# One core, a two-layer trunk in split float32: padded arrays, common splits, one turned K tile, and low parts that lag

## The chip, the cores and the metric

The kernel runs on one core of a Trainium2 chip. The metric is the device time of one execution in microseconds, and the runs shown are 2053.0, 2053.09 and 2053.85 us, a median of 2053.09 us. The profile is of one further execution.

## The reference, cut to what matters

256 tokens of width 2048 go through two layers. Layer 0 mixes with a short gated convolution, layer 1 with latent attention; each is followed by an MLP of width 8192, and each of the four sub-layers ends in a layer norm.

```python
def short_conv_mixer(x, w_in, conv_w, w_out):
    gate_b, gate_c, u = jnp.split(x @ w_in, 3, axis=-1)
    y = conv(gate_c * u, conv_w)                # depthwise, width 3, causal
    return (gate_b * y) @ w_out
def sq_relu_mlp(x, w1, w2):
    return jnp.square(jax.nn.relu(x @ w1)) @ w2
# per layer: h = LN(ALPHA*h + mix(h)); h = LN(ALPHA*h + sq_relu_mlp(h))
# layer 1's mix: multi-head latent attention, 16 heads, output projection w_o (2048 x 2048)
```

All inputs and the output are float32.

## The kernel before, in words

**Split products.** TensorE's one-pass float32 format drops bits, so each operand is split into a high part, which that format holds exactly, and a low part, the rest (`split`, L109 to L112: a cast on ScalarE, a subtraction on VectorE). A product needs high x high, high x low and low x high. Activations lie in SBUF as [128, 512] tiles per K tile: 256 columns of high parts, then 256 of low parts.

**Unit.** In `w_in`, `w_out`, `w_o` and `W1` a unit is one 128-wide block of output features over all 16 K tiles. Per K tile it issues two matmuls: `high` (L190) holds the weights' high part and streams 512 columns, `low` (L194) holds the weights' low part and streams 256. `mm_run` (L196) issues them in turn, h0 l0 h1 l1 and so on to h15 l15. One unit needs two stream halves of 512 KB. `products` (L230) yields the units; the convolution has 48, of which the first three run as a group that starts while data arrive, `w_out` has 16, `w_o` 16 (three in a group `first_o`, between the heads of attention), and each of W1's eight quarters q (`mlp`, L523) has 8 units. Quarter 0 uses another form (`mm_wide`, three 258-column matmuls per K tile, which fold in the layer norm).

**Down projection.** W2 is computed per quarter with the hidden activations as weights of TensorE and the rows of W2 as the 512-column moving operand. `down` (L259) does three matmuls per K tile, token half and column block (`dot`, L245 to L249). In the quarters of `FAST` (1 to 6 in layer 0, 1 to 7 in layer 1) half of the columns use a form with 7 instead of 8 block products (`down_fast`, L287), which needs sums of hidden blocks, `forms` (L566 to L574), and sums of weight blocks (`prepare`, L150 to L165).

**Order.** Weights are loaded by SyncE's queue (L132), split, and used; `take` (L171) runs `LOOK` = 5 halves ahead, with 5 raw buffers and 8 buffers each for high and low halves. A scheduler behind the tile framework fixes the order on each engine, and semaphores do the rest. PSUM has 8 banks.

**Where the arrays lie.** SBUF tiles follow each other in the order in which their pools were filled, rounded up to 32 bytes. Worked out from the sizes per partition: 16384 bytes of DMA scratch and 128 of constants, then `vec` 736, `cos_t` and `sin_t` 1024 each, `mask_t` 1536, `id_t` and `ones` 512 each, `col` 16 (32), `xres` 16384, and then the arrays a1 (16512), a2 (16512), b (33024) and c (16384), and behind them the raw, high and low buffers of 4096 each. So by 512 bytes a1 starts at remainder 384, a2 at 0, b at 128, c and all weight buffers at 384, and the small array `t4` of the fast form at 256. The convolution's input is in a1 and a2, its result z, W1's input and attention's output oT are in b, the hidden activations in c, the forms in a2.

**The hidden activations.** Per unit `hidden` (L558) evacuates PSUM, applies relu and square, and splits the 256 columns into `h` at once (`put_split`, L306). After each odd unit four subtractions and additions make the forms of the pair, which are split in turn (512 columns).

**The end.** In the last quarter of layer 1, `to_out` (L866) loads the norm's gain and bias, broadcast to all partitions, in four transfers of 512 KB (`gbt`, L869, GpSimd's queue). The array takes the place of W1's input, so they wait for the last W1 unit.

Of the kernel before, what the change touches and what calls it, by code (L numbers as in the profile page):

```python
# [15 lines left out]
P = 128  # L16
# [24 lines left out]

C_G, C_B, C_CW, C_QG, C_KG, C_END = 0, 64, 128, 176, 180, 184
# [3 lines left out]
def trunk(ctx: ExitStack, tc: tile.TileContext, xT, vecs, w_in, w_out, w_kv, w_q, w_uk, w_uv,  # L46
# [10 lines left out]


# [137 lines left out]
    def mm_run(wps, x, k0, k1, nk, tiles_first=False):  # L196
# [33 lines left out]
    def products(n, x, group=0, cuts=()):  # L230
# [20 lines left out]
    def held(x, t):  # L251

        return [x[:, o + t * P:o + (t + 1) * P] for o in (0, T)]
# [33 lines left out]
    def down_fast(x, forms):  # L287
# [3 lines left out]
        for j in range(n):  # L291
            b, = take(1)
            a = {"11": held(x[2 * j], 0), "12": held(x[2 * j + 1], 0), "22": held(x[2 * j + 1], 1)}
            for i in range(4):
                a[f"S{i + 1}"] = [forms[:, j, o, i * P:(i + 1) * P] for o in range(2)]
# [16 lines left out]
    vec = const.tile([P, C_END], F32, name="vec")  # L312
# [5 lines left out]
    col = const.tile([P, 4], F32, name="col")  # L318
# [28 lines left out]
    class Norm:  # L347
# [35 lines left out]
        def widen(self, *tags):  # L383
# [4 lines left out]
            for i, tag in enumerate(tags):  # L388
                x = act.tile([P, n, 2 * W], F32R, tag=tag, name=f"xd{self.idx}_{i}")
# [85 lines left out]
    xhl = [t[:, k, :] for t in [act.tile([P, NC // 2, 2 * T], F32R, tag=a, name=f"xhl0_{a}") for a in ("a1", "a2")]  # L475
           for k in range(NC // 2)]

    first = act.tile([P, 2 * GROUP, 1024], F32, tag="b", name="first")
# [14 lines left out]
    zt = act.tile([P, NC, 2 * T], F32R, tag="b", name="z")  # L493
    z = [zt[:, k, :] for k in range(NC)]
    cbuf = act.tile([P, 2, 5, T + 2], F32, tag="c", name="cbuf")
# [27 lines left out]
    def mlp(idx, ln, begin, blocks, fast):  # L523
# [3 lines left out]
        xt = act.tile([P, NC, 2 * T], F32R, tag="b", name=f"xhl{idx}")  # L527
# [20 lines left out]
        for q in range(NQ):  # L548
            ht = act.tile([P, QC, 2 * T], F32R, tag="c", name=f"h{idx}_{q}")
            h = [ht[:, k, :] for k in range(QC)]  # L550
            forms = None
            if q in FAST[idx // 2]:
                forms = act.tile([P, QC // 2, 2, 4 * P], F32R, tag="a2", name=f"forms{idx}_{q}")
            if q == NQ - 1:
                begin(block)
            pair = []

            def hidden(m, ps, evac, *func):  # L558
                f = tmp.tile([P, T], F32, tag="fh", name="fh", bufs=3)
# [4 lines left out]
                put_split(h[m], f)  # L564
                pair.append(f)
                if forms is not None and m % 2:  # L566
                    (a11, a21), (a12, a22) = ((v[:, :P], v[:, P:]) for v in pair[-2:])
# [417 lines left out]
```

## Time and profile before

| What | Value |
|---|---|
| Median of the runs | 2053.09 us |
| Profiled execution: span | 2049.4 us |
| Around the span, median less span | 3.7 us |
| TensorE busy | 2030.6 us (99%), 11208 matmul records |
| VectorE busy | 1662.8 us (81%) |
| ScalarE busy | 1194.1 us (58%) |
| DMA | 385.32 MB, 188 GB/s over the span |
| Granted TensorE clock, mean | 0.997 |

The matmul records overlap: a 512-column matmul has a record of some 390 ns but the next one starts some 230 ns later. So the busy share of TensorE says nothing about its pace; that is read from the starts of successive matmuls, either in the timeline or as the first and last start of the matmuls of one line in a stage, divided by the number of steps between them.

### The profile page before, as it was taken

Reading aid. Unit: us, or ns where it says so; the run is one execution under the profiler, and the core shown is the slowest. Engines: PE = TensorE matmul, PEld = TensorE weight load, DVE = VectorE, ACT = ScalarE, POOL = GpSimd, SP = SyncE. Lnnn points to the kernel's source line nnn. Section 1 sums busy time; section 2 is a strip of 40 time slices with the busy share of each in tenths; the row PEclk is TensorE's granted clock in tenths of the full one; section 3 lists DMA queues with packets and bytes.
Section 4 is the critical chain, followed back from the end, with each engine's and each line's share of the span. In section 5 each row is a group of like instructions: output and inputs, shape, how many; then the busy total and the mean of one; then the engine's idle time right before and its main releaser. Section 6 shows DMA issues by size and latency. Waiting matters only on the chain.

```text
span 2049.4 us, 30194 instructions
## 1 busy us (share of the span) xinstructions
PE 2030.6 (99%) x11208; PEld 1760.4 (86%) x11208; DVE 1662.8 (81%) x2602; ACT 1194.1 (58%) x1860; POOL 4.5 (0%) x25
## 2 busy tenths in 40 slices
PE   9999999999999999999999999999999999999997
PEld 8888888988888888888889998898888888888885
DVE  7667677678898988989788878776879888898988
ACT  6444445676566565655656665566656656566562
POOL 0000000000000000000000000000000000000000
PEclk9999999999999999999999999999999999999998
DMA  8666666564746557465755544656475664756653
GB/s 308 202 188 187 186 185 194 159 211 136 249 142 223 193 167 250 143 226 173 234 169 164 166 124 142 197 174 196 138 236 161 196 218 156 243 153 217 212 165 137
DMA packets 108003, 385.32 MB, mean 188 GB/s; under 512 B 11984, under 2 KB 13392, under 8 KB 107856
## 3 DMA queue, kind: packets, MB, share of 16 engines
q1 hardware_dynamic: 107136, 381.04, 58.7%
q0 software_dynamic: 576, 2.10, 0.3%
q8 instruction: 88, 1.44, 0.3%
q14 instruction: 59, 0.48, 0.1%
q10 hardware_dynamic: 144, 0.26, 0.0%
HBM read 381.25 MB, written 2.10 MB: 187 GB/s over the span
## 4 chain that ended last, share of the span: by engine, by line
PE 97%; DVE 1%; DMA 1%; issue 0%; ACT 0%; SPq 0%; DVEq 0%
PE ps_u L190 34%; PE ps_u L194 17%; PE ps_d L248 7%; PE ps_d L247 7%; PE ps_d L249 7%; PE ps_f L249 4%; PE ps_f L248 4%; PE ps_f L247 4%; PE ps_w L224 1%; PE ps_w L222 1%; PE ps_w L223 1%; PE ps_g L222 1%; PE ps_g L224 1%; PE ps_g L223 1%; PE ps_wo L190 1%; PE S L788 1%
## 5 line engine op out<-in xcount | busy, mean ns | idle before, releaser
L112 DVE TENSOR_TENSOR lo<-raw,hi 128x1024 fp32r<-128x1024 f32 x712 | 861.7, 1221 | 299.0 <-ACT hi L111 294.3
L111 ACT CAST hi<-raw 128x1024 fp32r<-128x1024 f32 x712 | 742.2, 1049 | 526.6 <-PE ps_u L190 289.5
L190 PE MATMUL ps_u<-xhl,hi 128*128 128x512 f32 x1792 | 632.2, 398 | 0.0
L194 PE MATMUL ps_u<-xhl,lo 128*128 128x256 f32 x1792 | 503.0, 281 | 0.0
L190 PEld LDWEIGHTS ps_u<-xhl,hi 128*128 128x128 f32 x1792 | 336.5, 188 | 82.3
L194 PEld LDWEIGHTS ps_u<-xhl,lo 128*128 128x128 f32 x1792 | 338.5, 189 | 0.5
L190 PE MATMUL ps_u<-xhl_a,hi 128*128 128x512 f32 x720 | 253.4, 396 | 0.0
L248 PE MATMUL ps_d<-lo,h 128*128 128x512 f32 x608 | 236.9, 390 | 0.0
L249 PE MATMUL ps_d<-hi,h 128*128 128x512 f32 x608 | 236.8, 390 | 0.0
L247 PE MATMUL ps_d<-hi,h 128*128 128x512 f32 x608 | 236.6, 389 | 0.0
L194 PE MATMUL ps_u<-xhl_a,lo 128*128 128x256 f32 x720 | 202.9, 282 | 0.0
L190 PEld LDWEIGHTS ps_u<-xhl_a,hi 128*128 128x128 f32 x720 | 135.2, 188 | 31.9
L194 PEld LDWEIGHTS ps_u<-xhl_a,lo 128*128 128x128 f32 x720 | 135.8, 189 | 0.0
L248 PEld LDWEIGHTS ps_d<-lo,h 128*128 128x128 f32 x608 | 114.1, 188 | 24.2 <-DVE lo L112 0.4
L247 PEld LDWEIGHTS ps_d<-hi,h 128*128 128x128 f32 x608 | 114.2, 188 | 24.0
L249 PEld LDWEIGHTS ps_d<-hi,h 128*128 128x128 f32 x608 | 114.1, 188 | 23.9
L111 ACT CAST hi_t<-raw_t 128x1024 fp32r<-128x1024 f32 x52 | 54.8, 1054 | 77.8 <-PE ps_u L190 41.8
L190 PE MATMUL ps_u<-z,hi 128*128 128x512 f32 x256 | 89.0, 392 | 0.0
L562 ACT ACTIVATE fh<-fh 128x256 f32<-128x256 f32 x112 | 46.4, 414 | 72.0 <-DVE fh L304 72.0
L222 PE MATMUL ps_w<-xd,hi 128*128 128x258 f32 x256 | 72.5, 284 | 0.0
L224 PE MATMUL ps_w<-xd,hi 128*128 128x258 f32 x256 | 72.5, 285 | 0.0
L223 PE MATMUL ps_w<-xd,lo 128*128 128x258 f32 x256 | 72.3, 282 | 0.0
(235 smaller groups left out, 3254.8 us busy)
## 6 DMA issues: line engine op xcount, KB each, us to landing
raw<-in_w_dram SPq DMA_DIRECT2D x408, 512.0 KB, 4.4
raw<-in_w2f_dram SPq DMA_DIRECT2D x104, 512.0 KB, 3.6
raw<-in_w_in_dram SPq DMA_DIRECT2D x90, 512.0 KB, 4.2
raw<-in_w_out_dram SPq DMA_DIRECT2D x32, 512.0 KB, 3.6
raw<-in_w_o_dram SPq DMA_DIRECT2D x32, 512.0 KB, 3.9
raw<-in_w_kv_dram SPq DMA_DIRECT2D x10, 512.0 KB, 4.3
raw<-in_w_q_dram SPq DMA_DIRECT2D x8, 512.0 KB, 4.5
raw<-in_w_uk_dram SPq DMA_DIRECT2D x8, 512.0 KB, 4.4
```

The lines of the kernel that those rows point to most:

```text
L111: nc.scalar.copy(hi, src)
L112: nc.vector.tensor_tensor(lo, src, hi.bitcast(F32), ALU.subtract)
L190: nc.tensor.matmul(ps, w[blk // 8][0][:, blk % 8, :], x, start=first, stop=False)
L194: nc.tensor.matmul(ps[:, :T], w[blk // 8][1][:, blk % 8, :], x[:, :T], start=False, stop=last)
L222: nc.tensor.matmul(ps[:, :W], hi, x[k][:, :W], start=k == 0, stop=False)
L223: nc.tensor.matmul(ps[:, :W], lo, x[k][:, :W], start=False, stop=False)
L224: nc.tensor.matmul(ps[:, :W], hi, x[k][:, W:], start=False, stop=k == NC - 1)
L247: nc.tensor.matmul(ps, x[0], w[0], start=first, stop=False)
L248: nc.tensor.matmul(ps, x[0], w[1], start=False, stop=False)
L249: nc.tensor.matmul(ps, x[1], w[0], start=False, stop=last)
L562: nc.scalar.activation(f, f, AF.Relu)
L788: nc.tensor.matmul(S[:, at:at + n], qp[:, tok], kp[:, :n], start=False, stop=True)
```

## The change

- `array` gives a1, a2, b and c rounded-up sizes (16896, 16896, 33280, 16384 bytes), `vec` and `col` are padded to 1024 and 512 bytes, `stats` to 320, and the DMA scratch shrinks from 16384 to 2048 bytes. By the same sum a1, a2, b, c, the weight and raw buffers, `t4` and the pair buffer `sf` all start at remainder 128 by 512 bytes.
- In the quarters 1 to 7 the relu and square of two units go into one pair buffer `sf` of 1024 columns, the four sums stand behind them there, and one split makes all 8 blocks (4 in layer 0's last quarter): high parts in c, low parts in a2. Nothing is split before the odd unit of a pair.
- In the first unit of each of these quarters the low matmul of K tile 2 stands before the high one: h0 l0 h1 l1 l2 h2 h3 l3.
- In the ungrouped units of the convolution, of `w_out` and of `w_o`, `mm_lag` issues h0 to h7, then h8 l0 h9 l1 to h15 l7, then l8 to l15.
- The four `gbt` transfers go to SyncE's queue.

```diff
+COL = 128
+LAG = 8
+    ROOM = {"a1": 16896, "a2": 16896, "b": 33280, "c": 16384}
+    def array(tag, dtype, name, *dims):
+        n = int(np.prod(dims))
+        t = act.tile([P, ROOM[tag] // 4], dtype, tag=tag, name=name)[:, :n]
...
         for k, (w, ps) in order:
+            if k == turn:
+                low(ps, w, k, x[k], False)
+                high(ps, w, k, x[k], False)
+                continue
             high(ps, w, k, x[k], k == 0)
             low(ps, w, k, x[k], k == nk - 1)
+    def mm_lag(ps, w, x):
+        for k in range(NC + LAG):
+            if k < NC:
+                high(ps, w, k, x[k], k == 0)
+            if k >= LAG:
+                low(ps, w, k - LAG, x[k - LAG], k == NC + LAG - 1)
...
-            mm_run([(w, ps)], x, 0, NC, NC)
+            if lag:
+                mm_lag(ps, w, x)
+            else:
+                mm_run([(w, ps)], x, 0, NC, NC, turn=turn if i == 0 else None)
...
+            forms = [array(a, F32R, f"h{idx}_{q}_{a}", QC // 2, 8 * P) for a in ("c", "a2")] if q else None
...
+                    if m % 2 == 0:
+                        state["pair"] = fast.tile([P, 8 * P], F32, tag="sf", name="sf")
+                    f = state["pair"][:, m % 2 * T:(m % 2 + 1) * T]
...
-                put_split(h[m], f)
...
+                    split(hi[:, :cols], lo[:, :cols], src[:, :cols])
...
-                for m, ps in enumerate(products(QC, xhl)):
+                for m, ps in enumerate(products(QC, xhl, turn=2, lag=False)):
...
-            nc.gpsimd.dma_start(gbt[:, n, :], gb[n].partition_broadcast(P))
+            nc.sync.dma_start(gbt[:, n, :], gb[n].partition_broadcast(P))
...
-    nc = _bacc.Bacc("TRN2", target_bir_lowering=False, num_devices=1)
+    nc = _bacc.Bacc("TRN2", target_bir_lowering=False, num_devices=1, dynamic_dma_scratch_size=2048)
```

More of the change, by code (lines that the diff above doesn't have):

```diff
@@ L294, in down_fast @@
             for i in range(4):
-                a[f"S{i + 1}"] = [forms[:, j, o, i * P:(i + 1) * P] for o in range(2)]
+                a[f"S{i + 1}"] = [v[:, j, (4 + i) * P:(5 + i) * P] for v in forms]
             for p, l, r in FACTORS:
@@ L523, in mlp @@
     def mlp(idx, ln, begin, blocks, fast):
-        xt = act.tile([P, NC, 2 * T], F32R, tag="b", name=f"xhl{idx}")
+        xt = array("b", F32R, f"xhl{idx}", NC, 2 * T)
         xhl = [xt[:, k, :] for k in range(NC)]
```

72 lines of the change are left out of this document (39 added, 33 removed).

## The prediction

> **What bounds the kernel now.** I read the page first: shares, chain, groups. In the chain's line the shares are of the span.
>
> ```profile
> span 2049.4 us, 30194 instructions
> PE 2030.6 (99%) x11208; PEld 1760.4 (86%) x11208; DVE 1662.8 (81%) x2602; ACT 1194.1 (58%) x1860; POOL 4.5 (0%) x25
> ...
> PE 97%; DVE 1%; DMA 1%; issue 0%; ACT 0%; SPq 0%; DVEq 0%
> ```
>
> TensorE is 97% of the chain, so hardly anything is to be had from waits, and time can only come from the pace at which matmuls follow each other. I therefore read the timeline of PE in two stages that do the same work: units of W1 in a middle quarter and in the last quarter of layer 0.
>
> ```profile
> 474.22 0.40 PE L190 MATMUL ps_u<-xhl,hi 128*128 128x512 f32 x1
> 474.46 0.28 PE L194 MATMUL ps_u<-xhl,lo 128*128 128x256 f32 x1
> 474.58 0.40 PE L190 MATMUL ps_u<-xhl,hi 128*128 128x512 f32 x1
> ...
> 475.28 0.40 PE L190 MATMUL ps_u<-xhl,hi 128*128 128x512 f32 x1
> ```
> ```profile
> 990.00 0.39 PE L190 MATMUL ps_u<-xhl,hi 128*128 128x512 f32 x1
> 990.23 0.28 PE L194 MATMUL ps_u<-xhl,lo 128*128 128x256 f32 x1
> 990.35 0.39 PE L190 MATMUL ps_u<-xhl,hi 128*128 128x512 f32 x1
> 990.58 0.28 PE L194 MATMUL ps_u<-xhl,lo 128*128 128x256 f32 x1
> 990.69 0.39 PE L190 MATMUL ps_u<-xhl,hi 128*128 128x512 f32 x1
> ```
>
> ```profile
> 458.70:503.90 45.20, 45.20 (x258) 39.18 (x256) 35.10 (x55) 28.67 (x50) 0.00 (x0) 1.00 0.44 138
> 978.00:1022.60 44.60, 44.60 (x259) 39.32 (x258) 32.16 (x49) 27.48 (x46) 0.00 (x0) 1.00 0.69 225
> ```
>
> The first column of the timeline is the start; the last three of the two stretches are granted clock, DMA share and GB/s. In the first stage three K tiles take 475.28 - 474.22 = 1.06 us, 353 ns each; in the second two take 0.69 us, 345 to 347 ns each. Same lines, arrays and shapes, clock at 1.00 in both: there are two **gaits**, a slow and a fast one. The rows of whole stages (count, then first and last start of L190) tell which stage has which: W1's second quarter in layer 0, its seventh and its last in layer 1, a stretch of the convolution, the most of `w_out`, and `w_o`.
>
> ```profile
> L190 PE MATMUL ps_u<-xhl,hi x128: 389/398/403, 458.7 to 503.5; 128*128 128x512 f32 x128
> L190 PE MATMUL ps_u<-xhl,hi x128: 389/398/403, 1856.1 to 1901.0; 128*128 128x512 f32 x128
> L190 PE MATMUL ps_u<-xhl,hi x128: 391/391/476, 1946.0 to 1990.2; 128*128 128x512 f32 x128
> L190 PE MATMUL ps_u<-xhl_a,hi x257: 387/396/403, 63.8 to 153.9; 128*128 128x512 f32 x129
> L190 PE MATMUL ps_u<-z,hi x209: 391/391/391, 295.0 to 367.1; 128*128 128x512 f32 x105
> L190 PE MATMUL ps_u<-oT,hi x208: 392/394/395, 1260.4 to 1332.2; 128*128 128x512 f32 x104
> ```
>
> Per K tile: 44.8/127 = 352.8 and 44.9/127 = 353.5 ns (I take 353.1); 44.2/127 = 348.0 with a disturbed first one in it; 90.1/256 = 352.0; 72.1/208 = **346.6**; 71.8/207 = 346.9. The six middle quarters of each layer come straight from 512-column matmuls of the down projection and keep the slow gait through all 128 K tiles. The two last quarters come from other matmuls (a mean, L365; transposes, L863) and keep the fast one. So the gait depends on how a stage is entered, and it lasts.
>
> Three more rows give the pace of one kind alone: 512 columns in the down projection (every third matmul is L248), 512 columns in the fast form (first matmuls of its four K pairs, 21 apart), and 256 columns (every third is L208).
>
> ```profile
> L248 PE MATMUL ps_d<-lo,h x64: 387/389/389, 415.4 to 458.2; 128*128 128x512 f32 x64
> L247 PE MATMUL ps_f<-t,h x4: 392/392/393, 503.9 to 518.5; 128*128 128x512 f32 x4
> L208 PE MATMUL ps_k<-lat,lo x16: 280/283/285, 1124.5 to 1129.9; 128*128 128x256 f32 x16
> ```
>
> 42.8/189 = **226.5** ns, 14.6/63 = **231.7** ns, 5.4/45 = **120** ns. And 226.5 + 120 = 346.5: the fast gait is the sum of the two kinds alone. I take that as the floor; no row is below it. The down projection has both operands at remainder 384 by 512 bytes; the fast form mixes weights of TensorE at 384 and 0 with moving operands at 384 and 256, and is 5.2 ns slower per matmul.
>
> **The change part by part.**
>
> *Turned K tile.* In 12 quarters the swap breaks the alternation after two K tiles. Price: none in instructions; both ends are zero (the gait is not left) and (353.1 - 346.6) x 126 x 12 = 9.8 us gained. Of the entries of other kinds that I see, W1's last quarters, `w_out` and `w_o` ended in the fast gait, the convolution in a slow one. I take the gain, **-9.5 us** with the first tiles left slow.
>
> *Padding.* With everything at remainder 128, the fast form should run as the down projection does, whose operands also agree. 84 matmuls x 5.2 ns x 12 blocks = 5.2 us; a few matmuls at each entry stay slow, **-5.0 us**. Both operands at 128 is in no row. But z and W1's input lie at 128 against weights at 384 and reach the floor, the down projection has 384 against 384 and is on it too, so I expect 128 and 384 to be alike. Bounds: 0, and -5.5.
>
> *Lag.* Eight h, then eight pairs, then eight l. At the floor it is the same sum as before, 8 x 226.5 + 8 x 346.6 + 8 x 120. The eight pairs are entered from 512-column matmuls, as W1's slow quarters are, so I price them slow: 8 x 6.5 = 52 ns, less some 7 because the first pair after such an entry is short, 45 ns a unit. The convolution now loses (352.0 - 346.6) x 16 = 86 ns in each of 45 units: gain 45 x 41 = 1.9 us. `w_out` and `w_o` lose nothing now: 29 x 45 = 1.3 us more. Net **-0.6 us**; bounds: all fast, -3.9; all 74 units as slow as W1, 74 x 104 ns - 3.9 = +3.8. The high matmul of the last K tile also comes 1.0 us earlier in the unit (8 x 226.5 + 7 x 346.6 = 4.2 us after its start, not 15 x 0.35), and `w_out`'s first unit needs z[15] there:
>
> ```profile
> 281.34 1.05 ACT L111 CAST hi<-raw 128x1024 fp32r<-128x1024 f32 x1 [1.40 <-PE ps_u L190]
> ...
> 283.57 0.42 DVE L309 TENSOR_TENSOR z<-cbuf,z 128x256 fp32r<-128x256 f32 x1
> ```
>
> The split that ends z stands behind a weight cast that waits for a high buffer and behind that weight's subtraction. With high parts first that buffer comes free about 0.9 us earlier, and in the new order on VectorE the z row stands ahead of that subtraction (1.2 us). So z[15] comes 1 to 2 us earlier too, and I take 0; without this cover it costs 1.0 us, once. Low buffers come free up to 1.8 us later; with 8 of them, four units' worth, nobody waits.
>
> *Common splits.* Per pair of hidden units ScalarE and VectorE each do one 1024-column split in place of three, and TensorE waits on none of it: the last pair is needed 63 matmuls, 14.3 us, after the last unit. In layer 0's last quarter it is needed 36 matmuls, 8.2 us, after it, and is ready now about 5.7 us after it:
>
> ```profile
> L309 DVE TENSOR_TENSOR h<-fh,h x2: 418/418/418, 1022.3 to 1027.9; 128x256 fp32r<-128x256 f32 x2
> ```
>
> The pair's split adds some 0.5 us: 2 us of cover, price **0**. The single pair buffer is rewritten behind the subtraction that reads it, on the same engine.
>
> *The gain and bias on another queue.* This is the one real stall. Rows: the chain of waits (load, start and length), the page (median of such loads), the timeline of VectorE, PE, GpSimd and SyncE, two stretches, then the block's own rows.
>
> ```profile
> 1993.17 8.60 DMA raw<-in_w2f_dram
> ```
> ```profile
> raw<-in_w2f_dram SPq DMA_DIRECT2D x104, 512.0 KB, 3.6
> ```
> ```profile
> 2001.80 1.23 DVE L154 TENSOR_TENSOR raw_t<-raw,raw 128x1024 f32<-128x1024 f32 x1 [3.39 <-DMA raw<-in_w2f_dram]
> 2002.94 0.28 DVE L573 TENSOR_TENSOR sf<-fh,sf 128x128 f32<-128x128 f32 x1
> ...
> 2005.61 0.68 DVE L112 TENSOR_TENSOR forms<-sf,forms 128x512 fp32r<-128x512 f32 x1
> ...
> 2006.15 0.50 PE L247 MATMUL ps_f<-t,h 128*128 128x512 f32 x1 [0.78 <-ACT t L111]
> 2008.08 0.55 PE L248 MATMUL ps_f<-t,h 128*128 128x512 f32 x1 [1.44 <-DVE t L112]
> ...
> 1990.99 2.23 POOL L869 DMA_DIRECT2D gbt<-in_gb_dram  x4 [1038.46 <-PE ps_u L194]
> 1988.47 5.03 SPq L132 DMA_DIRECT2D raw<-in_w2f_dram  x2
> ...
> 1993.00:2002.00 9.00, 9.00 (x41) 7.22 (x40) 5.07 (x10) 3.55 (x6) 0.21 (x1) 1.00 0.99 366
> 2008.00:2011.60 3.60, 3.52 (x9) 2.80 (x10) 3.41 (x4) 1.04 (x1) 0.00 (x0) 0.55 0.81 277
> ...
> L247 PE MATMUL ps_f<-t,h x4: 393/395/497, 1990.5 to 2006.1; 128*128 128x512 f32 x4
> ...
> L247 PE MATMUL ps_d<-hi,h x1: 389/389/389, 2014.4 to 2014.4; 128*128 128x512 f32 x1
> ```
>
> The last weight load of the fast form takes 8.6 us instead of 3.6, because the four transfers share the DMA engines with it (366 GB/s, share 0.99). TensorE waits for what is made of it, and then runs at half clock. The block lasts from 1990.5 to 2014.4, 23.9 us, where the same block takes 14.6/63 x 84 = 19.5: 4.4 us lost. After the change the four stand ahead of that load on SyncE. They wait for the same last unit (1991.0), and at 0.33 us each (the load's issue, 1993.17 to 1993.50) are out by 1992.3, before the load itself may start, so this wait delays nobody. 2.10 + 0.52 MB at 366 GB/s take 7.2 us, and the load lands at 1991.7 + 7.2 = 1998.9 instead of 2001.8. TensorE got its first operand 4.4 us and its second 6.3 us after the landing; of the latter 0.28 + 0.68 us, the last pair's forms, now stands ahead of the load's work. So they come by 2003.3 and 2004.2, and TensorE asks at 1990.5 + 14.3 = 2004.8. The stall goes, and the half clock with it: **-4.4 us**. Bounds: 0 if the load gets no earlier, and -4.9.
>
> The Trainium skill ("DMA: Bandwidth & Descriptors", Queues, rings and completion order) has each DMA engine alternate between queues packet by packet; the 8.6 us agree with it.
>
> **Sum** against the profiled execution: 9.5 + 5.0 + 0.6 + 4.4 = 19.5 us off a span of 2049.4, so 2029.9; the median of the runs is 3.7 us above that span, which gives **2033.6 us**.
>
> **Rivals.** *The swap does not change the gait.* The entry from the down projection led to the slow gait in 12 of 12 quarters, and I have no row of l l h h without a wait beside it. Then 9.5 us stay: 2043.
>
> *The lagged pairs run fast.* Then the convolution gains 3.9 and the others lose nothing: 2030.3.
>
> *The load gets no earlier* (the four transfers slower on this queue): 2038.
>
> *Order and place do not matter.* In the Trainium skill ("TensorE: Matmul & The Clock Gate", Part 2) the streamed operand and the weight load have read ports of their own, so that a weight load steals nothing, and matmuls follow at N/2.4 + 2.5 ns. As a mechanism here: gaits come from events outside the kernel's order, and only the stall goes, 2048.7. The two timelines above speak against it: one work, one clock, 353 and 346 ns.
>
> *Slower: the common remainder locks.*
>
> ```profile
> L248 PE MATMUL ps_d<-lo,h 128*128 128x512 f32 x608 | 236.9, 390 | 0.0
> ```
>
> If operands both at 128 hold every stage in the gait of the fast form, the 3 x 608 = 1824 matmuls of the down projection go from 226.5 to 231.7 (+9.5), W1's two last quarters and `w_out`, `w_o` go slow (256 + 464 K tiles x 6.5 = +4.7), nothing comes from swap or padding, the stall still goes (-4.4): 2063. It turns the sign once a 512-column matmul costs over 2.4 ns more in the down projection. Against it: operands that agree at 384 run at the floor.
>
> **How the numbers follow.** Forecast 0.55 (2033.6; 2030 to 2037). Swap without effect 0.22, lag fast 0.08, load no earlier 0.05, only the stall 0.05, lock 0.05. The range 2029 to 2045 takes in the first four, 0.90; a tenth of that I leave for terms that are mis-sized beyond it. About 0.2% (4.1 us) is what a measurement here can tell from no change: faster 0.91, same 0.04, slower 0.05.
>
> **What would show it.** Right: L190 in W1's middle quarters spans 44.0 us over 127 K tiles, not 44.8; the fast form's four first matmuls lie 14.3 us apart, not 14.6; no wait of PE near the end and a clock of 1.00 there; 5.59 us between units of the convolution, down from 5.63. Wrong: the 353 ns gait after the swap, a PE wait for `z` or for h, a down projection above 226.5 ns.

## The result, and the profile after

The changed kernel takes **2035.48 us** (median of four runs, 2034.64 to 2035.57) against 2053.32 us (2053.0 to 2053.85) before: a ratio of 0.9909, 95% interval 0.9895 to 0.9923. Its profiled execution took 2034.64 us, 2.1 us more than its span. The page of that execution (span, engines, chain):

```profile
span 2032.5 us, 30055 instructions
PE 2015.7 (99%) x11208; PEld 1759.8 (87%) x11208; DVE 1653.1 (81%) x2494; ACT 1181.7 (58%) x1752; POOL 2.3 (0%) x21
PE 96%; DVE 2%; DMA 1%; issue 1%; ACT 0%; DVEq 0%; ACTq 0%
```

As before, TensorE is nearly the whole chain, so the 16.9 us that the span lost must be in its pace. I read first the rows of whole stages after the change (`high` is now L201; first and last start of the row): W1's second quarter in layer 0, its last in layer 0, its seventh and its last in layer 1.

```profile
L201 PE MATMUL ps_u<-xhl,hi x128: 389/391/400, 458.5 to 502.5; 128*128 128x512 f32 x128
L201 PE MATMUL ps_u<-xhl,hi x128: 391/398/586, 970.1 to 1015.2; 128*128 128x512 f32 x128
L201 PE MATMUL ps_u<-xhl,hi x128: 389/391/400, 1843.6 to 1887.7; 128*128 128x512 f32 x128
L201 PE MATMUL ps_u<-xhl,hi x128: 391/391/481, 1932.4 to 1976.5; 128*128 128x512 f32 x128
```

44.0/127 = 346.5 and 44.1/127 = 347.2 ns per K tile in the middle quarters, where it was 353: the swap put them in the fast gait. The second row is the surprise: 45.1/127 = 355 ns (353 behind its first K tile, which took 542). That quarter was fast before, and the swap has made it slow. The timeline of PE shows both around the swapped K tile ("x2" is the pair of low or of high matmuls that the swap puts side by side), first W1's second quarter:

```profile
458.84 0.40 PE L201 MATMUL ps_u<-xhl,hi 128*128 128x512 f32 x1
459.07 0.40 PE L205 MATMUL ps_u<-xhl,lo 128*128 128x256 f32 x2
459.31 0.63 PE L201 MATMUL ps_u<-xhl,hi 128*128 128x512 f32 x2
...
460.60 0.39 PE L201 MATMUL ps_u<-xhl,hi 128*128 128x512 f32 x1
...
460.95 0.39 PE L201 MATMUL ps_u<-xhl,hi 128*128 128x512 f32 x1
...
461.29 0.39 PE L201 MATMUL ps_u<-xhl,hi 128*128 128x512 f32 x1
```

And layer 0's last quarter, in the same view:

```profile
970.14 0.59 PE L201 MATMUL ps_u<-xhl,hi 128*128 128x512 f32 x1
...
970.92 0.40 PE L205 MATMUL ps_u<-xhl,lo 128*128 128x256 f32 x2
971.15 0.63 PE L201 MATMUL ps_u<-xhl,hi 128*128 128x512 f32 x2
...
971.73 0.40 PE L201 MATMUL ps_u<-xhl,hi 128*128 128x512 f32 x1
...
972.08 0.40 PE L201 MATMUL ps_u<-xhl,hi 128*128 128x512 f32 x1
...
972.44 0.40 PE L201 MATMUL ps_u<-xhl,hi 128*128 128x512 f32 x1
...
972.79 0.40 PE L201 MATMUL ps_u<-xhl,hi 128*128 128x512 f32 x1
```

In the first, the K tiles follow at 0.35 and 0.34 us; in the second at 0.35, 0.36 and 0.35, and so on to its end. By the trace's start times in full, the slow gait is a pattern of three: K tiles of 349, 350 and 361 ns in turn, 353 on average. One order, two outcomes; the entries differ. Ahead of the swap K tile 1 took 350 ns in the first (slow) and 347 in the second (fast).

The fast form's first matmuls of its four K pairs, as in the prediction:

```profile
L273 PE MATMUL ps_f<-t,h_c x4: 389/389/391, 502.9 to 517.2; 128*128 128x512 f32 x4
```

(517.2 - 502.9)/63 = 227.0 ns, against 231.7: the fast form now runs at the pace of the down projection. The last block in the chain of waits:

```profile
1979.93 7.49 DMA raw<-in_w2f_dram
1987.45 1.24 DVE raw_t L165
...
1991.26 1.15 DVE lo L123
...
1992.45 0.50 PE ps_f L274
```

The one wait that the timeline of PE still marks there:

```profile
1992.45 0.50 PE L274 MATMUL ps_f<-lo,h_c 128*128 128x512 f32 x1 [0.21 <-DVE lo L123]
```

And the block as a stretch (its length, PE busy; behind POOL the clock, DMA share and GB/s):

```profile
1976.84:1996.80 19.96, 19.75 (x86) 15.54 (x85) 18.08 (x24) 12.33 (x17) 0.00 (x0) 1.00 0.72 255
```

The load still takes 7.49 us, yet TensorE waits 0.21 us instead of 2.2 (0.78 and 1.44), the clock is 1.00 throughout, and the block lasts 19.96 us instead of 23.86. That is still 0.88 us over the 19.08 of the other blocks: the records of matmuls overlap, so that a start that is 0.1 us late shows as no idle time, and five more matmuls of the last K pair follow at 0.27 to 0.35 us instead of 0.23.

Stage by stage, from a stage's first matmul to the next stage's first, in the profiled executions of before, after, and the runs below (us; the convolution in its two parts, before and behind the mean in its middle):

| Stage | before | after | no swap | no lag | no padding | two starts | swaps for lag |
|---|---|---|---|---|---|---|---|
| W1, each of 12 middle quarters | 45.21 | 44.39 | 45.21 | 44.39 | 44.39 | 44.39 | 44.39 |
| W1, last quarter, layer 0 | 44.57 | 45.39 | 44.57 | 45.39 | 45.39 | 44.57 | 44.57 |
| W1, last quarter, layer 1 | 44.46 | 44.48 | 45.30 | 44.48 | 44.49 | 44.48 | 44.48 |
| Fast form, each of 12 (the twelfth 19.17 after, 19.11 without lag) | 19.50 | 19.08 | 19.10 | 19.08 | 19.44 | 19.08 | 19.08 |
| Fast form, last block | 23.86 | 19.96 | 20.22 | 19.87 | 20.20 | 19.98 | 19.82 |
| Convolution, 24 units | 134.97 | 134.57 | 134.55 | 135.67 | 133.47 | 133.44 | 133.14 |
| Convolution, 21 units | 118.35 | 117.92 | 117.92 | 116.67 | 117.01 | 117.02 | 116.67 |
| `w_out`, 16 units | 89.03 | 89.71 | 89.71 | 90.58 | 89.69 | 88.96 | 89.01 |
| `w_o`, 13 units | 72.11 | 72.88 | 72.88 | 73.49 | 72.90 | 72.28 | 72.13 |

Before to after: middle quarters -9.8, layer 0's last quarter +0.8, fast form -5.0, its last block -3.9, the lagged stages +0.6 (-0.8, +0.7, +0.8), the last down projection -0.2, the other down projections -0.55 in sum. TensorE's last matmul ends 17.75 us earlier; the end follows 0.87 us later behind it than before (13.74 against 12.87 us), since VectorE's last sums, and not that matmul, set the end.

### The profile page after: what moved, and what is told of

It reads as the page before. It is cut to its first block, busy times and chain, and to the rows that moved or that the text cites. A ratio compares the mean times of both kernels' runs of the same rounds, so it can differ in the third digit from the quotient of the medians.

```text
span 2032.5 us, 30055 instructions
## 1 busy us (share of the span) xinstructions
PE 2015.7 (99%) x11208; PEld 1759.8 (87%) x11208; DVE 1653.1 (81%) x2494; ACT 1181.7 (58%) x1752; POOL 2.3 (0%) x21
## 3 DMA queue, kind: packets, MB, share of 16 engines
q8 instruction: 88, 1.44, 0.3%
## 4 chain that ended last, share of the span: by engine, by line
PE 96%; DVE 2%; DMA 1%; issue 1%; ACT 0%; DVEq 0%; ACTq 0%
PE ps_u L201 33%; PE ps_u L205 17%; PE ps_d L273 7%; PE ps_d L274 7%; PE ps_d L275 7%; PE ps_f L274 4%; PE ps_f L275 4%; PE ps_f L273 4%; PE ps_w L247 1%; PE ps_w L245 1%; PE ps_w L246 1%; PE ps_g L245 1%; PE ps_g L247 1%; PE ps_g L246 1%; PE ps_g L201 1%
## 5 line engine op out<-in xcount | busy, mean ns | idle before, releaser
L201 PE MATMUL ps_u<-xhl,hi 128*128 128x512 f32 x1792 | 622.1, 392 | 0.0
L201 PEld LDWEIGHTS ps_u<-xhl,hi 128*128 128x128 f32 x1792 | 334.4, 187 | 73.1
L201 PE MATMUL ps_u<-xhl_a,hi 128*128 128x512 f32 x720 | 211.1, 394 | 0.0
L273 PE MATMUL ps_d<-hi,h_c 128*128 128x512 f32 x480 | 186.8, 390 | 0.0
L274 PE MATMUL ps_d<-lo,h_c 128*128 128x512 f32 x480 | 186.6, 389 | 0.0
L275 PE MATMUL ps_d<-hi,h_a 128*128 128x512 f32 x480 | 186.6, 389 | 0.0
L201 PEld LDWEIGHTS ps_u<-xhl_a,hi 128*128 128x128 f32 x720 | 132.4, 188 | 27.6
L205 PE MATMUL ps_u<-xhl_a,lo 128*128 128x256 f32 x720 | 144.4, 282 | 0.0
L275 PEld LDWEIGHTS ps_d<-hi,h_a 128*128 128x128 f32 x480 | 90.1, 188 | 18.8
L274 PEld LDWEIGHTS ps_d<-lo,h_c 128*128 128x128 f32 x480 | 90.1, 188 | 18.7 <-DVE lo L123 0.2
L273 PEld LDWEIGHTS ps_d<-hi,h_c 128*128 128x128 f32 x480 | 90.1, 188 | 18.7
L274 PE MATMUL ps_f<-lo,h_c 128*128 128x512 f32 x208 | 81.2, 390 | 0.2 <-DVE lo L123 0.2
L275 PE MATMUL ps_f<-hi,h_a 128*128 128x512 f32 x208 | 81.1, 390 | 0.0
L273 PE MATMUL ps_f<-hi,h_c 128*128 128x512 f32 x208 | 80.7, 389 | 0.0
L201 PE MATMUL ps_u<-z,hi 128*128 128x512 f32 x256 | 75.0, 394 | 0.0
```

What stands on the lines that cost most here:

```text
L201: nc.tensor.matmul(ps, w[blk // 8][0][:, blk % 8, :], x, start=first, stop=False)
L205: nc.tensor.matmul(ps[:, :T], w[blk // 8][1][:, blk % 8, :], x[:, :T], start=False, stop=last)
L273: nc.tensor.matmul(ps, x[0], w[0], start=first, stop=False)
L274: nc.tensor.matmul(ps, x[0], w[1], start=False, stop=False)
L275: nc.tensor.matmul(ps, x[1], w[0], start=False, stop=last)
```

## The experiments

Times are medians; each ratio is to runs of the kernel before on the same chip. The chips differ (that kernel took 2051.3 to 2054.4 us on them), so across chips the ratios and the stages compare, and not the times. The theory I started from: the swap, the padding and the lag each act on the pace alone and add up; the last block is a matter of when a load lands. Its rival: the gait is an accident of how a stage is entered, and neither order nor place decides it.

**No swap.** The changed kernel without the turned K tile.

```diff
-                for m, ps in enumerate(products(QC, xhl, turn=2, lag=False)):
+                for m, ps in enumerate(products(QC, xhl, turn=None, lag=False)):
```

> The changed kernel with the swap of K tile 2 taken out of W1's first units, nothing else. Theory (the swap alone moves W1 from the slow to the fast gait): the twelve middle quarters go back from 44.39 to 45.2 us each, +9.8 us, and layer 0's last quarter, which the swap seems to have pushed into the slow gait (45.39 us), goes back to 44.57, -0.8: about 2044.5 us. Rival (the padding or the common splits made W1 fast, the swap does nothing): 2035.5 us and quarters of 44.4 us.

Measured: 2044.87 us, ratio 0.9959 [0.9940, 0.9979]. The same quarter as above:

```profile
L201 PE MATMUL ps_u<-xhl,hi x128: 389/398/403, 458.6 to 503.4; 128*128 128x512 f32 x128
```

44.8/127 = 353 ns, in all 12 middle quarters. The swap alone takes them out of the slow gait; the equal starts that the padding gives don't. Layer 0's last quarter is fast again, and layer 1's, which entered another way here, is slow without it.

**No lag.** The default of `lag` is turned off; the call for W1 sets its own and stays as it is.

```diff
-    def products(n, x, group=0, cuts=(), turn=None, lag=True):
+    def products(n, x, group=0, cuts=(), turn=None, lag=False):
```

> The changed kernel with the lag taken out: all units of the convolution, w_out and w_o issue high and low in turn; W1 keeps its swap. Theory (the lag only breaks the gait anew in every unit, and costs about 60 ns a unit over the floor wherever it is): each of the three stages then has one gait throughout. All three fast: 2.9 + 1.0 + 0.8 us less, 2031 us; all slow (107 ns a unit, 74 units): 3.3 us more, 2039 us; w_o was fast before and should be fast (72.1 us). Rival (the lag itself saves time, by fewer changes between 256 and 512 columns): over 2039 us, with stages above 5.65 us a unit.

Measured: 2036.25 us, ratio 0.9919 [0.9890, 0.9947]. L201 in the convolution's two parts:

```profile
L201 PE MATMUL ps_u<-xhl_a,hi x378: 395/398/403, 26.8 to 160.0; 128*128 128x512 f32 x189
L201 PE MATMUL ps_u<-xhl_a,hi x336: 392/395/577, 160.6 to 276.9; 128*128 128x512 f32 x168
```

Some records are missing, so I divide by K tiles of whole units: 135.67/384 = 353.3 ns in the first part, 116.67/336 = 347.2 in the second, in one stage of one kernel with one order, parted by a 0.2 us mean. Without the lag, what a stage takes hangs on how it is entered: `w_out` and `w_o`, fast before, ran slow here (90.58, 73.49), so that the lag saves 1.3 us in these stages against this run and costs 0.6 against the kernel before.

**No padding.** The arrays where they lay before (a1 at remainder 384 by 512, a2 at 0, the weights at 384), all else as changed.

```diff
-COL = 128
+COL = 4
-    ROOM = {"a1": 16896, "a2": 16896, "b": 33280, "c": 16384}
+    ROOM = {"a1": 16512, "a2": 16512, "b": 33024, "c": 16384}
-    vec = const.tile([P, 2 * P], F32, name="vec")[:, :C_END]
+    vec = const.tile([P, C_END], F32, name="vec")
...
-        stats = small.tile([P, 2, NB, 10], F32, tag="stats", name="stats", bufs=1)[:, :, :, :6]
+        stats = small.tile([P, 2, NB, 6], F32, tag="stats", name="stats", bufs=1)
```

> The changed kernel with the old sizes of a1, a2, b, vec, col and stats, so that the arrays start at remainders 384, 0, 128, 384 by 512 bytes again and the high and low hidden parts lie at 384 and 0; common splits, swap and lag stay. Theory (remainders that differ cost 5 ns in a 512-column matmul): the fast form goes back to 19.5 us a block, +0.42 x 13 = 5.4 us, and the down projection, whose weights now alternate between 384 and 0, loses up to the same 5 ns in each of 1440 matmuls, up to 7 us: 2041 to 2048 us. Rival (the common splits or the new layout of the forms made the fast form faster): 2035.5 us, blocks of 19.1 us.

Measured: 2043.64 us, ratio 0.9957 [0.9937, 0.9976]. The fast form's first matmuls, and L201 in the convolution's first part:

```profile
L273 PE MATMUL ps_f<-t,h_c x4: 393/395/395, 501.4 to 516.0; 128*128 128x512 f32 x4
L201 PE MATMUL ps_u<-xhl_a,hi x378: 389/392/398, 26.7 to 157.5; 128*128 128x512 f32 x189
```

14.6/63 = 231.7 ns: the loss in the fast form is back, 0.36 us a block, and the down projection's blocks with hidden high and low parts at different starts lose 0.43 each as well. So it was the padding, not the common splits.

It is not, though, that the two operands of one matmul must start alike. In `w_out` and `w_o` of this run the streams start at 128 and the weights at 384, and the stages take 89.69 and 72.90 us, as with all at 128 (89.71, 72.88). The runs of nine high matmuls between two lagged units show it in the timeline of PE, first here in `w_out`, then in the changed kernel's convolution:

```profile
304.09 2.22 PE L201 MATMUL ps_u<-z,hi 128*128 128x512 f32 x9
306.15 0.28 PE L205 MATMUL ps_u<-z,lo 128*128 128x256 f32 x1
```
```profile
102.22 1.25 PE L205 MATMUL ps_u<-xhl_a,lo 128*128 128x256 f32 x9
103.30 2.22 PE L201 MATMUL ps_u<-xhl_a,hi 128*128 128x512 f32 x9
105.36 0.28 PE L205 MATMUL ps_u<-xhl_a,lo 128*128 128x256 f32 x1
```

Both take 2.06 us. Where 4 to 5 ns a matmul were lost, a start changes from one matmul to the next: in the fast form, and in this run's down projection, where the streams stay at 384 and only the held hidden parts go between 384 and 0 (22.19 us a block, 231 ns a matmul). So the rows speak for the change of starts as the cost; how it costs is not shown.

But the lagged convolution is *faster* without padding, 133.47 and 117.01 us: in each of its pairs the high matmul streams from a2 (remainder 0) and the low one from a1 (384). That asked for a run of its own (two starts, below).

**Gain and bias on SyncE in the kernel before.**

```diff
-            nc.gpsimd.dma_start(gbt[:, n, :], gb[n].partition_broadcast(P))
+            nc.sync.dma_start(gbt[:, n, :], gb[n].partition_broadcast(P))
```

> The kernel before with one edit: the four transfers of the norm's gain and bias go to SyncE's queue. Theory (sharing the DMA engines with the last load of the fast form made the stall and the half clock): the last block of the fast form takes 19.5 to 19.9 us instead of 23.9, 2049.1 us. Rival (the stall went because the common splits shortened VectorE's list): 2053.3 us, block of 23.9 us.

Measured: 2051.09 us, ratio 0.9991 [0.9980, 1.0002]; inconclusive by time alone, since `w_out` fell into the slow gait in this run (90.63 against 89.03). The last block took 21.05 us instead of 23.86; the 19.5 to 19.9 that were expected were missed. Its load in the chain of waits:

```profile
1995.58 8.80 DMA raw<-in_w2f_dram
2004.40 1.24 DVE raw_t L154
```

And the block as a stretch with the same columns:

```profile
1992.88:2013.93 21.05, 20.02 (x87) 15.65 (x85) 17.71 (x23) 11.52 (x17) 0.00 (x0) 1.00 0.73 252
```

The load took 8.80 us on the new queue, not less: ahead of it in its queue stand the four transfers now, and each byte still has to pass. What helped is that VectorE had the last pair's forms done at 2002.5 us, while it waited for the load (they stood behind it before), so TensorE idled 1.0 us instead of 2.2, and the clock stayed at 1.00. Of the 3.9 us that the changed kernel gains in this block the queue alone thus gives 2.8, with the splits as they were; the starts give 0.4, as in the other blocks; the last 0.7 are not taken apart, and the common splits may have part in them.

**Swap scan.** Each quarter has its swap at another K tile: 1 to 7 in layer 0, 7 to 13 in layer 1.

```diff
-                for m, ps in enumerate(products(QC, xhl, turn=2, lag=False)):
+                for m, ps in enumerate(products(QC, xhl, turn=q if idx == 1 else q + 6, lag=False)):
```

> The changed kernel with the swapped K tile at another place in each quarter of W1: in layer 0's quarters at K tile 1, 2, ... 7, in layer 1's at K tile 7, 8, ... 13 (the changed kernel has K tile 2 in all). The theory (phase): in the slow gait every third K tile is the long one (241 and 120 ns), and entered from the down projection those are K tiles 2, 5, 8, 11; the swap frees the gait only where it falls on one of them, so the middle quarters with K tile 2, 5, 8, 11 last 44.4 us (plus 6.7 ns for each slow K tile ahead of the swap, under 0.1 us) and the others stay at 45.2 us, or all quarters of one remainder by three act alike. Then some 8 of the 12 middle quarters lose 0.8 us and the time is about 2042 us. The rival (any swap frees it): all middle quarters 44.4 us, time 2035.5 us.

Measured: 2043.01 us, ratio 0.9950 [0.9930, 0.9970]. L201 in layer 0's middle quarters, swap at K tile 1, 2, 3, 4, 5, 6:

```profile
L201 PE MATMUL ps_u<-xhl,hi x128: 387/398/403, 459.3 to 504.2; 128*128 128x512 f32 x128
L201 PE MATMUL ps_u<-xhl,hi x128: 389/391/400, 545.4 to 589.4; 128*128 128x512 f32 x128
L201 PE MATMUL ps_u<-xhl,hi x128: 389/398/403, 630.6 to 675.5; 128*128 128x512 f32 x128
L201 PE MATMUL ps_u<-xhl,hi x128: 387/398/403, 716.7 to 761.5; 128*128 128x512 f32 x128
L201 PE MATMUL ps_u<-xhl,hi x128: 389/391/403, 802.7 to 846.8; 128*128 128x512 f32 x128
L201 PE MATMUL ps_u<-xhl,hi x128: 389/398/403, 888.0 to 932.9; 128*128 128x512 f32 x128
```

Slow, fast, slow, slow, fast, slow; in layer 1 slow at 7, 9, 10 and 12, fast at 8 (44.43 us) and 11 (44.45). Only K tiles 2, 5, 8, 11 free the gait, each three later for 0.02 us more: the slow K tiles ahead of it. In the slow gait of these quarters K tiles 2, 5, 8 and 11 are the long ones of 361 ns; the swap has to fall on one of them. The two last quarters fit: layer 0's, fast where nothing is swapped, was made slow by its swap at K tile 7 (45.37 us), and layer 1's, entered slow, was not freed by one at K tile 13 (45.29). This is the most telling run of the study.

**Another common start.** All arrays at remainder 256 instead of 128.

```diff
-COL = 128
+COL = 160
```

> The changed kernel with the common start of all padded arrays moved by 128 bytes: the columns start at 256 bytes past a multiple of 512 in place of 128. The theory (it is the agreement of the operands' starts that sets the pace of the fast form, not the place where they agree): the fast form's first blocks stay at 19.1 us and the time at 2035.5 us. The rival (a start of 128 is special): the fast form goes back to 19.4 to 19.5 us a block, 12 times, and the time is 2040 us; the down projection may leave 226.5 ns a matmul, which costs 1.8 us for each ns.

Measured: 2035.21 us, ratio 0.9912 [0.9892, 0.9932]; fast form 19.08 (its twelfth block 19.80, with a wait), middle quarters 44.39. The common starts 128 and 256 do alike. The two last quarters changed sides: 44.59 us in layer 0, 45.29 in layer 1.

```profile
L201 PE MATMUL ps_u<-xhl,hi x128: 391/391/585, 970.5 to 1014.7; 128*128 128x512 f32 x128
L201 PE MATMUL ps_u<-xhl,hi x128: 393/398/478, 1932.6 to 1977.6; 128*128 128x512 f32 x128
```

Behind the wait, layer 0's quarter was entered in the slow gait here (K tile 1 took 233 and 118 ns) and the swap freed it; in the changed kernel it was entered in the fast one (230 and 117 ns), and the swap kicked it out. In layer 1 it was the other way round. The swap thus turns the gait over in both directions, as the scan says.

**Two starts.** The lag stays; the second half of the convolution's input, of z and of oT starts 384 bytes further on, so that in a lagged pair the high matmul's stream starts at 0 and the low one's at 128; no swap in layer 0's last quarter.

```diff
...
+        at = [k * 2 * T + 96 * (k >= NC // 2) for k in range(NC)]
...
-                for m, ps in enumerate(products(QC, xhl, turn=2, lag=False)):
+                for m, ps in enumerate(products(QC, xhl, turn=None if (idx, q) == (1, NQ - 1) else 2, lag=False)):
```

> The changed kernel with two edits. The swap is left out of layer 0's last quarter, where it set the slow gait. The second half of the K tiles of the convolution's input, of z and of oT starts 384 bytes further on (at a multiple of 512), while the first half stays at 128, so that in a lagged pair the high matmul's and the low matmul's operands have different starts, as they had in the convolution of the run without padding, where the loss was 0.88 us in place of 2.89. The theory (it was this difference that made those pairs fast): the convolution loses 0.9 us over the floor (2.0 less than the changed kernel), the w_out stage 0.3 (0.7 less), the w_o stage 0.3 (0.5 less), and the last quarter 0.8 less: 2031.5 us. The rival (it was something else in that run, such as the entry): the three stages stay at 2.9, 0.96 and 0.77 us, and only the last quarter gains: 2034.7 us.

Measured: 2031.32 us, ratio 0.9893 [0.9873, 0.9913]. L207 (`high`) in the convolution's first part and in layer 0's last quarter:

```profile
L207 PE MATMUL ps_u<-xhl_a,hi x377: 389/392/398, 26.6 to 157.2; 128*128 128x512 f32 x189
L207 PE MATMUL ps_u<-xhl,hi x128: 391/391/586, 967.6 to 1011.8; 128*128 128x512 f32 x128
```

The three stages lose 0.85, 0.21 and 0.17 us over the floor, as expected from the run without padding; by the trace's start times in full a lagged unit takes 5560 ns instead of 5607, with a floor of 5547. It is the difference between the two streams that does it: in the run without padding, `w_out` and `w_o` had both streams at 128 and only the weights elsewhere, and gained nothing. So a change of starts, which makes 512-column matmuls slower, makes these pairs faster; why is not settled.

**Swaps in the place of the lag.** One swapped K tile where the run without lag had its long one, and none in layer 0's last quarter.

```diff
...
-            if lag:
-                mm_lag(ps, w, x)
-            else:
-                mm_run([(w, ps)], x, 0, NC, NC, turn=turn if i == 0 else None)
+            mm_run([(w, ps)], x, 0, NC, NC, turn=turn if i == (group if at_unit is None else at_unit) else None)
...
-    pss = products(3 * NC, xhl, GROUP, (2, 4, 8, 12))
+    pss = products(3 * NC, xhl, GROUP, (2, 4, 8, 12), turn=2)
-    summed(ln, products(NC, z), residual)
+    summed(ln, products(NC, z, turn=2, at_unit=1), residual)
-        yield from products(NC - WO_G, oT)
+        yield from products(NC - WO_G, oT, turn=2)
...
-                for m, ps in enumerate(products(QC, xhl, turn=2, lag=False)):
+                for m, ps in enumerate(products(QC, xhl, turn=None if (idx, q) == (1, NQ - 1) else 2)):
```

> The changed kernel with no lag anywhere: in its place one swapped K tile (K tile 2) in the first unit of the convolution, in the second unit of the w_out stage and in the first unit of the w_o stage behind the first group; the swap is left out of layer 0's last quarter. In the run without lag these stages ran slow from such entries with the long K tile at K tile 2: 135.7 us the convolution's first part, 90.6 w_out, 73.5 w_o. The theory (one swap on the long K tile frees the gait in any stage, until a wait or another order sets it again): 133.2, 88.9 and 72.2 us, the last quarter of layer 0 44.6 us; the time 2036.25 - 2.5 - 1.7 - 1.3 - 0.8, about 2030 us. The rival (the swap works only behind the down projection): the three stages stay as without lag, and the time is 2035.4 us.

Measured: 2030.42 us, ratio 0.9891 [0.9874, 0.9907].

```profile
L201 PE MATMUL ps_u<-xhl_a,hi x380: 390/391/391, 26.7 to 158.1; 128*128 128x512 f32 x190
L201 PE MATMUL ps_u<-z,hi x249: 391/391/499, 277.8 to 364.0; 128*128 128x512 f32 x125
L201 PE MATMUL ps_u<-oT,hi x197: 391/391/391, 1253.7 to 1321.6; 128*128 128x512 f32 x197
```

133.14, 89.01 and 72.13 us: the three stages are within 0.3 us of the floor. One swap does what the lag could not.

**Gain and bias late.** The version with the swaps, with the four transfers held back until the last down projection's first sum.

```diff
-            nc.sync.dma_start(gbt[:, n, :], gb[n].partition_broadcast(P))
...
+                nc.vector.tensor_copy(gbt[0][:, :, 0], block(n, t)[:, :NB])
+                for i in range(NB):
+                    nc.gpsimd.dma_start(gbt[0][:, i, :], gb[i].partition_broadcast(P))
```

> The version with the swapped K tiles in the place of the lag, and one more edit: the four transfers of the gain and bias go out at the very end, on GpSimd's queue, held back by a copy of 128x4 numbers into their buffer that VectorE makes behind the first sum of the last down projection; so nothing of them shares the DMA engines with the last weight load of the fast form. The theory (in the runs with the four on SyncE's queue ahead of it that load still took 7.2 to 8.8 us, because all transfers under way share the engines, and the rest of the wait in the last block is this): the load takes 3.5 to 5 us, the last block of the fast form 19.1 to 19.3 us in place of 19.8 and the last down projection 21.8 in place of 21.95; the time is 2029.5 us. The rival (the wait comes from VectorE's queue, not from the load): the block stays at 19.8 us and the time at 2030.4 us. A third possibility is that the gain and bias land too late for the last normalization (from about 2014 us on), then the end comes later by what is missing, 1 to 5 us.

Measured: 2032.51 us, ratio 0.9891 [0.9874, 0.9907]; a miss of 3 us in the time, though the ratio is that of the swaps' run. The last block took 19.08 us, with no wait, and its load 3.49 us: the company of the four transfers was the cause. But the four now left at 2011.16 and held the norm up at 2015 (0.8 us), the last down projection took 22.65 us, and the convolution's first part ran slow (L201's row, then VectorE's timeline):

```profile
L201 PE MATMUL ps_u<-xhl_a,hi x382: 387/398/403, 26.8 to 161.3; 128*128 128x512 f32 x191
```

```profile
2015.45 0.75 DVE L923 SCALAR_TENSOR_TENSOR u<-acc,mv,gbt 128x512 f32<-128x512 f32 x1 [0.80 <-DMA gbt<-in_gb_dram]
```

Its code there is that of the run above. Its first units, which the loads of the start pace, left it at another phase (K tile 1 took 348 ns, not 350), and the swap on K tile 2 fell on a short one. The profile is of the slowest of its four executions, 2034.11 us; the quickest took 2030.54.

**The changed kernel again, and the swaps again.**

> The changed kernel itself once more, on the same chip as the version before, so that the two are compared side by side. Every theory: 2035.5 us, and in the trace 45.4 us for W1 in layer 0's last quarter and 44.4 us in the twelve middle quarters, if the gait follows from the entry and the order alone.

> The version with the swap in the place of the lag once more. In the last version, which has the same convolution, the convolution's first part took 135.65 us where this one had 133.14, behind first units that the loads of the start had paced otherwise. The theory (the swap frees the gait only where it falls on the long K tile, and at the start the loads decide where that is): the first part takes either 133.1 or 135.7 us in this run, nothing between, and the time is 2030.4 or 2032.9 us; behind waits of the kernel's own (w_out, w_o, W1) the pace is as before: 89.0, 72.1 and 44.4 us. The rival (the first run's 133.14 follows from the order alone): 133.14 us and 2030.4 us.

Measured: 2035.88 us, ratio 0.9911 [0.9896, 0.9926], and 2030.87 us, ratio 0.9900 [0.9884, 0.9916]. The stages of the changed kernel agree with its first profile to 0.03 us, except at the start, in the twelfth block of the fast form (19.10 against 19.17) and at the end (last block 20.47 against 19.96, last down projection 22.39 against 22.00). In the swaps' version the convolution took 133.14 us once more, so three profiled executions of that code gave 133.14, 133.14 and 135.65: no value between, and one that went the other way. That speaks against the rival of a pace set by the order alone; the gait of executions without a profile is not known (those of the second run took 2029.58 to 2035.62 us).

**Lag, two starts, and the transfers a little earlier.** The version with two starts, the four transfers behind a copy from the fast form's sums.

```diff
-        for n in range(NB):
-            nc.sync.dma_start(gbt[:, n, :], gb[n].partition_broadcast(P))
...
+        nc.vector.tensor_copy(gbt[:, :, 0], block(0, 0)[:, :NB])
+        for n in range(NB):
+            nc.gpsimd.dma_start(gbt[:, n, :], gb[n].partition_broadcast(P))
```

> The version that keeps the lag and gives the two halves of the operands different starts, with no swap in layer 0's last quarter, and the four transfers of the gain and bias on GpSimd's queue behind a copy that waits for the fast form's last block, some 12 us earlier than in the last version. The theory (the last load's company is what keeps TensorE waiting there, and the lagged pairs with different starts do not depend on how a stage is entered): the convolution 133.4 and 117.0 us, w_out 88.96, w_o 72.28 as in the earlier run of this version; the last block of the fast form 19.1 in place of 20.0, the last down projection 21.8, and the gain and bias in time; about 1.1 us less than 2031.3, so 2030.2 us. The rival (the last down projection or the end loses what the block gains, as in the last version): 2031.3 us or more.

Measured: 2030.58 us, ratio 0.9896 [0.9879, 0.9912]. The block and the last down projection as stretches:

```profile
1972.96:1992.05 19.09, 19.09 (x87) 15.78 (x86) 18.03 (x25) 13.29 (x18) 0.00 (x0) 1.00 0.57 169
1992.05:2014.86 22.81, 22.23 (x97) 17.76 (x95) 21.90 (x37) 4.79 (x6) 2.23 (x4) 1.00 0.46 159
```

And the wait that took the old one's place, in the timeline of PE:

```profile
2004.34 0.50 PE L280 MATMUL ps_d<-lo,h_c 128*128 128x512 f32 x1 [0.58 <-DVE lo L129]
```

The block is at its floor, 19.08 us; TensorE comes into the down projection 0.9 us sooner, meets VectorE in the sums of the fast form, and waits 0.58 us for a weight split that stands behind them. The down projection takes 22.81 us where it took 21.97 with two starts: the gain is given back. The rival was right about the stages; that the time is under its 2031.3 us goes with another chip (ratio 0.9896 against 0.9893) and an end that follows the last matmul 0.6 us sooner.

This version, the two with swaps and the two starts have the lowest ratios of the study, 0.9891 to 0.9900, against 0.9909 and 0.9911 for the changed kernel. All these intervals overlap. On one chip, though, the two starts (2030.57 to 2032.08 us) and the swaps (2029.83 to 2031.79) lie clear of the run at 256 (2034.90 to 2035.52), which has the changed kernel's order; among each other the times don't rank them. By the stage table the two starts save 4.2 us and the swaps 5.0 against the changed kernel.

## Why the prediction was right, and where it was not

The forecast was 2033.6 us, the time 2035.48: the case that was forecast, 1.9 us off. By its steps:

- **Turned K tile**, -9.5: measured -9.8 in the middle quarters. The reason given (the swap breaks the alternation) was too weak: in eight of twelve quarters of the scan it broke the alternation and freed nothing. That K tile 2 was one of the four right ones was not in my argument: that was luck, and with eight of twelve places of no effect the chance of 0.22 for "no effect" was low.
- **Layer 0's last quarter**, not priced: +0.8. I counted the swap as nothing where the gait was fast already. It turns such a gait over: this is the step that failed.
- **Padding**, -5.0: measured -5.0, shown to be the padding by the run without it, and not bound to the place by the run at 256. The reason given, that a matmul's two operands agree, is not what the runs show: weights at 384 under a stream at 128 run at the floor, as my own rows of z and W1's input said, and what costs is starts that change from matmul to matmul. The padding took both away.
- **Lag**, -0.6: measured +0.6. The eight pairs run slow, as I said, but the term was mis-sized: 60 ns a unit, not 45 (134.57/24 = 5607 ns against a floor of 5547). By the start times in full the pairs lose 37 ns; 20 more go to the first three high matmuls behind the low ones (235, 233 and 231 ns instead of 227; in the rows above, nine take 2.06 us and not 2.04), which I had put at nothing without a reason, and the rest to the low ones. So the convolution gained 0.8, not 1.9, and the output projections lost 1.45, not 1.3.
- **Common splits**, 0: nothing waits for them where I looked. In the last block the last pair's work now stands ahead of the load's, but the queue alone does that too (gain and bias on SyncE in the kernel before), so no gain is shown for them.
- **Gain and bias**, -4.4: measured -3.9 in the block, of which 0.4 belongs to the padding. Near in size, wrong in the working: the load took 7.49 us, not 5.7, and landed 10.6 us behind the block's start, against 11.3 before and not 8.4. The queue moved the landing little; VectorE's order did the rest. That the load's company was the cause of what remained is shown by the last two versions: without it the block has no wait. The Trainium skill ("DMA: Bandwidth & Descriptors", Queues, rings and completion order) has the descriptors of one ring consumed in order. The 7.49 and 8.80 us of a load behind four transfers in one queue agree with that. They don't tell it from mere sharing, which gave 8.60 us with the four on another queue.
- **Around the span**, 3.7: it was 2.1 us in the profiled execution, and the median lay 0.8 us above that execution. In the runs of the kernel before that have both numbers the time is 1.7 to 1.9 us over the span, so half of the 3.7 was that the profiled execution had been a quick one. The span was missed by 2.6 us (2032.5 for 2029.9), the time by less.

The terms that failed add to 0.8 + 1.2 + 0.5 us, 0.9 us were lost behind the last matmul, and 1.0 us came better than foreseen in the middle quarters (0.3) and the down projections (0.2 in the last, 0.55 in the others); that is the 2.6 us but for 0.2. Of the rivals, "order and place do not matter" is out: eight quarters of the scan differ from four by the place of one pair alone, and the run without padding from the changed kernel by addresses. The locking of the common remainder didn't show: the down projection kept 226.7 ns.

## What to carry to other kernels

Where one stage runs at two paces with the same work and clock, read its start-to-start times over a dozen matmuls before changing anything: the pattern (here two short steps and a long one) tells where a swap acts, and a swap in the right place is worth more than a new order. Such a state hangs on how the stage is entered, so leave out the swap where the stage is already fast, and look at each stage in the trace rather than at the sum. Where a wait at the end is taken away, look at what its engine meets next: here VectorE's sums took back what the load gave.

## What the runs showed of the hardware

- The pace of alternating 512- and 256-column matmuls has two steady states, 346.6 and 353 ns per pair, at a clock of 1.00. Each held for up to 384 K tiles (the convolution's first part, slow without lag, fast with the swap). One swapped pair turned it over in both directions, and a stage's entry set either; no run shows what makes it.
- With starts that stay the same by 512 bytes from matmul to matmul, 512-column matmuls followed each other at 227 ns: all at 128, 256 or 384, or streams at 128 over weights at 384. With starts that change it was 231 to 231.7. For lagged units the opposite was measured where the high and the low stream start apart, 13 ns a unit lost against 60. No run shows why.
- Two waits close together, 2.2 us in all, were followed by half the clock for 3.4 us in the kernel before; waits of 1.0 us in one block (gain and bias on SyncE) left it at 1.00.
